# Block sums after the transposes: four transposed blocks in place of seven operands, and the third MLP pair's first products among the first pairs'

## The chip, the cores and the metric

The kernel runs on one core of a Trainium2 chip. The metric is the device time of one execution in microseconds (us), given as the median of several runs; a profiled execution of the same kernel gives the views that are read here. The engines are TensorE (PE; its weight loads are shown as PEld), VectorE (DVE), ScalarE (ACT), GpSimd (POOL) and SyncE (SP), which here issues nearly all transfers. Work of TensorE lands in PSUM, in banks of 128 x 512 float32; everything else lies in SBUF.

## The reference

One decoder block in float32: x is 1024 tokens by 1024 channels.

```python
proj = x @ w_in                      # 1024 x 7168: q, f, i, og, pool_v, gate_a, gate_b
a = HGRN2(q, f, i) -> per-head RMSNorm * sigmoid(og) -> @ w_a
b = per-group linear(causal_mean_w(pool_v) - pool_v) * pool_scale
mix = (sigmoid(gate_a) * a + sigmoid(gate_b) * b) @ w_out
x = LN(alpha * x + mix)
x = LN(alpha * x + relu(x @ w_up)^2 @ w_down)
```

HGRN2 is a gated recurrence over the tokens, 8 heads of 128 channels. The up projection of the MLP has 4096 columns.

## The kernel before, in words

**Seven products for eight.** Each large product of x is computed in the form of Strassen and Winograd. The tokens are split in two halves of 512, the channels in two halves of 512. So x is four blocks a11, a12 (first tokens) and a21, a22 (second tokens). Four sums are formed: s3 = a11 - a21, s2 = a22 - s3, s1 = a21 + a22, s4 = a12 - s2. A pair of output blocks then needs seven half-size products, with a11, a12, s3, a22, s2, s1 and s4, in place of eight (`pair`, with the parts p1 to p7 for the products and t1 to t4 for the sums of weight blocks).

**Precision.** A float32 operand is split into a high part, which ScalarE casts (`A.copy`, fp32r), and a low part, which VectorE gets by subtraction. Three products, high by high, high by low and low by high, make one product (`prod`, `three`). So each operand tile of 128 x 512 costs one ScalarE and one VectorE instruction, and each product of 512 x 128 x 512 costs twelve TensorE instructions.

**Transposes.** Tokens lie on the partitions as loaded, and a product wants the channels there. `transposed_parts` (line 152) turns four 128 x 128 squares into one PSUM bank by four TensorE transposes (line 156), and `split_into` (lines 117 and 118) splits it straight from there into an operand tile. `first_tokens` does so for a11 and a12, `second_tokens` for s3, a22, s2, s1 and s4. The sums are made before the transposes, in `row_sums`, on rows of tokens (lines 169 to 182), one generator per tile of 128 tokens; it yields between the sums so that they can be placed among other work.

**The two stages with x as operand.** The first stage, about the first 96 us, projects the values i. There the weights move and x stands as the stationary operand; products go down four chains of PSUM banks (`onto_chain`) or row by row through the two "hg" banks (`by_rows`). Sums of rows are placed by `summed()` between the products. After it come the heads, with gates and pooling in between, and the products with w_a and w_out. The second stage begins where the layer norm ends (about 800 to 906 us): `mix` forms rows of the sum, norms them and stores them, `row_sums` follows for tiles 4 to 6 directly and for tile 7 later, then the MLP's pairs of hidden units start. The first two pairs go through the seven products together (`run_second`), because each new operand has just become ready; the other fourteen run one after another. The third pair's weight blocks lie in a pool, `fw`, that opens when the pool of rows closes, and its results take rooms there (`spare`).

**Order.** Instructions are written in the program's order and a planner places them on each engine; `tc.issue_after` holds instructions behind another one, `tc.high_priority` draws them forward. Each engine, SP's queue of transfers too, runs its own instructions strictly in the order so made. `ps_tile(tag)` hands out PSUM banks: four "pj", two "hg", two "tr".

Of the kernel before, what the change touches and what calls it, by code (L numbers as in the profile page):

```python
# [16 lines left out]
P = 128  # L17
# [25 lines left out]
def tile_hybrid_block(  # L43
# [40 lines left out]
    def act_tile():  # L84

        return act.tile([P, 2, HALF], F32R, tag="act", name=nm("act"))
# [65 lines left out]
    def transposed_parts(tiles, off, name, kp, tag):  # L152

        ps = ps_tile(tag, 2)
        for c in range(CH):
            done = PE.transpose(ps[:, c * P : (c + 1) * P], tiles[c][:, off + kp * P : off + (kp + 1) * P], ident)  # L156
# [4 lines left out]
    s3_rows = [None] * CH  # L161

    def row_sums(t):


        a11, a12 = r[t - CH][:, :HALF], r[t - CH][:, HALF:]
        a21, a22 = r[t][:, :HALF], r[t][:, HALF:]
        if s3_rows[t - CH] is None:
            V.tensor_add(s1_rows[t - CH], a21, a22)
            s3_rows[t - CH] = a21  # L170
            own = False
        else:
            s1_rows[t - CH] = a21
            own = True
        s3 = s3_rows[t - CH]
        yield V.tensor_sub(s3, a11, a21).ins
        V.tensor_sub(a11, a22, s3)
        yield
        if own:
            V.tensor_add(a21, a21, a22)  # L180
        yield
        V.tensor_sub(a12, a12, a11)
        yield

    def first_tokens(*names):
        for name in names:
            for kp in range(CH):
                transposed_parts(r[:CH], HALF if name == "a12" else 0, name, kp, "tr")

    def second_tokens(name, *tags):  # L190
        where = dict(s2=(r[:CH], 0), s3=(s3_rows, 0), s1=(s1_rows, 0), a22=(r[CH:], HALF), s4=(r[:CH], HALF))
        tiles, off = where[name]
        return [transposed_parts(tiles, off, name, kp, tags[kp % len(tags)]) for kp in range(CH)]
# [66 lines left out]
    def pair(raw, rooms, takes, pz_tag="pj", twin=False):  # L260


        b11, b12, b21, b22 = (raw[kh][:, :, n] for kh in range(2) for n in range(2))
# [36 lines left out]
        def p2(w):  # L300
            ps["c"] = ps_tile()
            prod(ps["c"], w, "a12", True)
# [67 lines left out]
    def run_second(pairs, sums, begun=False):  # L370

        def later(name, *tags, summed=False, after=None):
            def made():
                if summed:
                    with tc.issue_after(made_last[after]) if after else nullcontext():
                        for one in sums:
                            next(one)
                second_tokens(name, *tags)
            return made

        made = (
            ((lambda: None) if begun else later("s3", "tr", "hg", summed=True), later("a22", "tr")),
            (later("s2", "tr", summed=True, after="s3"),), (later("s1", "tr", summed=True, after="a22"),), (later("s4", "tr", summed=True, after="s2"),), (),
        )
        run(*(p[2:] for p in pairs), made=made, behind=(None, "s3", None, None, None))
# [10 lines left out]
    s1_rows = [None] * CH  # L396
    wq = w_scope.enter_context(tc.tile_pool(name="wq", bufs=1, side="right", reuse_waits="tile"))
    with tc.tile_pool(name="xr", bufs=8, side="right", reuse_waits="tile") as xr:
# [5 lines left out]
        ps = ps_tile("tr", 2)  # L404
# [20 lines left out]
        s3_rows[:] = [xr.tile([P, HALF], F32, tag="s3", name=nm("s3"), bufs=CH) for _ in range(CH)]  # L425
# [71 lines left out]
        c11, c21, c22 = ([None] * CH for _ in range(3))  # L497

# [10 lines left out]
        def take_p4(c, ps):  # L509
            c21[c] = c_late()  # L510
            V.tensor_add(c21[c], c22[c], ps)

        def take_p6(c, ps):
            V.tensor_add(c21[c], c21[c], ps)
            put(1, 0, c, c21[c])
# [10 lines left out]
        def made(name):  # L526
            second_tokens(name, "tr")

        sums = [row_sums(t) for t in range(CH, 8)]

        def summed():
            for one in sums:
                next(one)

        first_tokens("a11")
        w = parts(b11)
        first_tokens("a12")
# [4 lines left out]
        made("s3")  # L542
# [5 lines left out]
        made("a22")  # L548
        by_rows(w, "s3", copied(c22, lambda: xr.tile([P, HALF], F32, tag="s3", name=nm("s3"), bufs=CH)))
        with behind_parts("s3"):  # L550
            for k in range(CH):
                V.tensor_add(b22[k], b22[k], b11[k])
                V.tensor_sub(b21[k], b21[k], b22[k])
            w = parts(b21)
            summed()
        made("s2")
        by_rows(w, "a22", take_p4)
        with behind_parts("a22"):
            w = parts(b22)
            summed()  # L560
        made("s1")
        onto_chain(w, "s2", False, take_p6)
        with behind_parts("s2"):
            for k in range(CH):
                V.tensor_sub(b12[k], b12[k], b11[k])
            w = parts(b12)
            again = wide_rows()
            load_block(again, 1, 1)
            b22 = rows_of_block(again)
            summed()  # L570
        made("s4")
# [47 lines left out]
    with tc.tile_pool(name="tmp", bufs=1, side="right", reuse_waits="tile") as tmp:  # L619
# [19 lines left out]
        def head_inputs(h):  # L639
# [23 lines left out]
            ))  # L663
# [278 lines left out]
        nxt = head_inputs(0)  # L942
# [134 lines left out]
    s1_rows[:] = [c_tile() for _ in range(CH - 1)] + [None]  # L1077
    s3_rows[:] = [None] * (CH - 1) + [c_tile()]
    with tc.tile_pool(name="wo", bufs=1, side="right", reuse_waits="tile") as mp:
# [11 lines left out]
        def mix(t, cc):  # L1091
# [22 lines left out]
        first_tokens("a11", "a12")  # L1114
# [18 lines left out]
    with tc.tile_pool(name="up", bufs=1, side="right", reuse_waits="tile") as up:  # L1133
# [15 lines left out]
        def units(i, raw):  # L1149
# [28 lines left out]
            return pair(raw, (c_tile,) * 3, (take(0), last, take(2), take(3)), "hg", i < 2)  # L1178

        def up_blocks(i):  # L1180
            return w_blocks(w_up, i * 2 * P, i * 2 * P + P, (raw_tile, up_raw_tile, lambda: room_raw.pop())[2 if i == 2 else i % 2])
# [5 lines left out]
        sums = row_sums(7)  # L1187
# [11 lines left out]

        room_raw = [ws0[0][:, n : n + 1].rearrange("p m (k n c) -> p (m k) n c", k=CH, n=2) for n in range(2)]  # L1200
        for i in range(2, NP):
            raw, load = up_blocks(i)
            if i == 2:
                spare[:] = [ws0[1][:, n // 2, n % 2 * HALF : (n % 2 + 1) * HALF] for n in range(7)]
# [189 lines left out]
```

## Time and profile before

| | us |
|---|---|
| median of three runs (lowest, highest) | 1477.53 (1477.52, 1479.11) |
| profiled execution | 1482.98 |
| its span, first to last instruction | 1481.3 |
| busy: TensorE, weight loads, VectorE, ScalarE | 1459.1, 1210.8, 1144.8, 746.5 |
| mean granted clock of TensorE | 0.996 |

Rows of a group give the line, the engine, the operation, the tile written and the tiles read, the count, the busy time, the mean of one in ns and the engine's idle time before it, with what ended it. Rows of waits read "engine and its instruction <- what it waited for: us in all, times, longest". Rows of a stretch give its length, then the busy time of PE, PEld, DVE, ACT and POOL with counts, the granted clock, the share of the transfer engines and GB/s. Rows in order of time start with the start and the duration in us; those of the chain of work give start, time on the chain, engine, tile and line.

### The profile page before, as it was taken

Reading aid. Unit: us, or ns where it says so; the run is one execution under the profiler, and the core shown is the slowest. Engines: PE = TensorE matmul, PEld = TensorE weight load, DVE = VectorE, ACT = ScalarE, POOL = GpSimd, SP = SyncE. Lnnn points to the kernel's source line nnn. Section 1 sums busy time; section 2 is a strip of 40 time slices with the busy share of each in tenths; the row PEclk is TensorE's granted clock in tenths of the full one; section 3 lists DMA queues with packets and bytes.
Section 4 is the critical chain, followed back from the end, with each engine's and each line's share of the span. In section 5 each row is a group of like instructions: output and inputs, shape, how many; then the busy total and the mean of one; then the engine's idle time right before and its main releaser. Section 6 shows DMA issues by size and latency. Waiting matters only on the chain.

```text
span 1481.3 us, 20065 instructions
## 1 busy us (share of the span) xinstructions
PE 1459.1 (99%) x7113; PEld 1210.8 (82%) x7113; DVE 1144.8 (77%) x1845; ACT 746.5 (50%) x1365; POOL 63.9 (4%) x244
## 2 busy tenths in 40 slices
PE   8999999999999999999999999999999999999997
PEld 7888888888888887777888887888888888888886
DVE  5867998999998786578985787666666887777977
ACT  4445565665557556355542165555555533343435
POOL 0001110011011010000002100000000100000000
PEclk9999999999999999999999999999999999999999
DMA  6142223233333436996664134444464774545422
GB/s 242 60 140 86 81 85 125 81 95 102 99 114 100 164 124 221 318 296 224 212 198 171 55 102 164 145 152 151 157 229 162 283 264 134 165 131 181 129 71 114
DMA packets 159557, 226.79 MB, mean 153 GB/s; under 512 B 11200, under 2 KB 83424, under 8 KB 159456
## 3 DMA queue, kind: packets, MB, share of 16 engines
q1 hardware_dynamic: 157520, 218.93, 44.5%
q0 software_dynamic: 1152, 4.19, 0.7%
q10 hardware_dynamic: 784, 2.38, 0.5%
q8 instruction: 56, 0.92, 0.3%
q14 instruction: 45, 0.37, 0.1%
HBM read 154.16 MB, written 71.30 MB: 152 GB/s over the span
## 4 chain that ended last, share of the span: by engine, by line
PE 93%; DMA 3%; DVE 2%; ACT 1%; issue 1%; SPq 0%; DVEq 0%; ACTq 0%
PE ps_pj L201 16%; PE ps_pj L199 16%; PE ps_pj L200 15%; PE ps_pj L1275 4%; PE ps_pj L1277 4%; PE ps_pj L1276 4%; PE ps_hg L199 2%; PE ps_hg L201 2%; PE ps_hg L200 2%; PE ps_pj L99 2%; PE ps_pj L101 2%; PE ps_pj L100 2%; PE ps_tr L156 1%; PE ps_hg L1275 1%; PE ps_hg L1277 1%; PE ps_hg L1276 1%
## 5 line engine op out<-in xcount | busy, mean ns | idle before, releaser
L199 PE MATMUL ps_pj<-act,w 128*128 128x512 f32 x1072 | 419.8, 394 | 5.3 <-DVE q L725 2.0
L200 PE MATMUL ps_pj<-act,w 128*128 128x512 f32 x1072 | 419.5, 391 | 0.0
L201 PE MATMUL ps_pj<-act,w 128*128 128x512 f32 x1072 | 414.9, 392 | 1.9 <-DVE w L113 1.7
L199 PEld LDWEIGHTS ps_pj<-act,w 128*128 128x128 f32 x1072 | 201.3, 188 | 49.5 <-ACT w L112 2.9
L201 PEld LDWEIGHTS ps_pj<-act,w 128*128 128x128 f32 x1072 | 201.3, 188 | 45.3 <-DVE w L113 4.3
L200 PEld LDWEIGHTS ps_pj<-act,w 128*128 128x128 f32 x1072 | 201.4, 188 | 40.4
L112 ACT CAST w<-t 128x512 fp32r<-128x512 f32 x170 | 104.5, 620 | 128.5 <-PE ps_pj L200 65.5
L112 ACT CAST w<-raw 128x512 fp32r<-128x512 f32 x143 | 88.1, 620 | 117.9 <-PE ps_pj L200 53.7
L113 DVE TENSOR_TENSOR w<-t,w 128x512 fp32r<-128x512 f32 x170 | 115.9, 687 | 34.5 <-ACT w L112 27.7
L113 DVE TENSOR_TENSOR w<-raw,w 128x512 fp32r<-128x512 f32 x143 | 97.7, 688 | 57.3 <-ACT w L112 41.8
L1237 ACT CAST act<-act 128x1024 fp32r<-128x1024 f32 x66 | 67.0, 1050 | 110.9 <-issue 35.0
L1238 DVE TENSOR_TENSOR act<-act,act 128x1024 fp32r<-128x1024 f32 x66 | 79.5, 1221 | 18.8 <-ACT act L1237 18.8
L1276 PE MATMUL ps_pj<-act,act 128*128 128x512 f32 x240 | 92.9, 389 | 0.0
L1277 PE MATMUL ps_pj<-act,act 128*128 128x512 f32 x240 | 92.9, 389 | 0.0
L1275 PE MATMUL ps_pj<-act,act 128*128 128x512 f32 x240 | 92.5, 389 | 0.0
L272 DVE TENSOR_TENSOR c<-c,ps_pj 128x512 f32<-128x512 f32 x95 | 64.6, 680 | 31.4 <-PE ps_pj L201 25.8
L199 PE MATMUL ps_hg<-act,w 128*128 128x512 f32 x160 | 62.8, 397 | 0.5 <-ACT room L268 0.5
L268 ACT COPY c<-ps_pj 128x512 f32<-128x512 f32 x95 | 54.6, 584 | 17.1 <-PE ps_pj L201 14.7
L200 PE MATMUL ps_hg<-act,w 128*128 128x512 f32 x160 | 63.1, 395 | 0.0
L201 PE MATMUL ps_hg<-act,w 128*128 128x512 f32 x160 | 62.8, 392 | 0.0
L813 DVE RECIPROCAL tC<-tA 128x128 f32<-128x128 f32 x64 | 54.6, 909 | 0.0
L117 ACT CAST act<-ps_tr 128x512 fp32r<-128x512 f32 x54 | 31.0, 590 | 46.8 <-PE ps_tr L156 46.7
(361 smaller groups left out, 2707.5 us busy)
## 6 DMA issues: line engine op xcount, KB each, us to landing
h<-c SPq DMA_DIRECT2D x105, 256.0 KB, 2.6
act<-h SPq DMA_DIRECT2D x78, 256.0 KB, 2.9
raw<-in_w_in_dram SPq DMA_DIRECT2D x64, 256.0 KB, 3.4
draw<-in_w_down_dram SPq DMA_DIRECT2D x16, 1024.0 KB, 8.1
raw<-in_w_up_dram SPq DMA_DIRECT2D x30, 512.0 KB, 4.3
raw<-in_w_in_dram SPq DMA_DIRECT2D x18, 512.0 KB, 3.7
hf<-h SPq DMA_DIRECT2D x34, 256.0 KB, 2.9
c<-o SPq DMA_DIRECT2D x24, 256.0 KB, 4.2
```

The costliest lines, as they stand in the source:

```text
L112: A.copy(hi, src)
L113: V.tensor_sub(lo, src, f(hi))
L199: PE.matmul(ps, wh[:, k], th, start=first and k == 0, stop=False, skip_group_check=True)
L200: PE.matmul(ps, wh[:, k], tl, start=False, stop=False, skip_group_check=True)
L201: PE.matmul(ps, wl[:, k], th, start=False, stop=k == CH - 1, skip_group_check=True)
L268: A.copy(t, ps)
L272: V.tensor_add(t, t, ps)
L1237: A.copy(hi, src)
L1238: V.tensor_sub(lo, src, f(hi))
L1275: PE.matmul(ps, hh[:, w], wh, start=fresh and n == 0, stop=False, skip_group_check=True)
L1276: PE.matmul(ps, hh[:, w], wl, start=False, stop=False, skip_group_check=True)
L1277: PE.matmul(ps, hl[:, w], wh, start=False, stop=n == M - 1, skip_group_check=True)
```

## The change

`transposed` now only transposes. `in_parts` splits any tile, in PSUM or SBUF, into an operand. `first_tokens` transposes a11 and a12, splits them and copies them with ScalarE into `xt`. `second_tokens` transposes for s3 (the block a21) and for a22 only; the sums s3, s2, s1 and s4 are formed by VectorE in place on the transposed tiles of `xt` and split from there. `row_sums` and the generators go. In the first stage the transposes of a11 go to the banks "tr", "tr", "hg", "hg" (in the loop over names: all "tr" before) and the idle products at the start take "hg"; results c21 and c22 lie in rows of x that are no longer needed, and three conditions on the order are put on the evacuations of p4 and p6. In the MLP the third pair loads its blocks into the left halves of rows 4 to 7 once these are transposed, its first product runs after the first step of the first two pairs and its second after two more, and its rooms are the right halves of rows.

```diff
-    def transposed_parts(tiles, off, name, kp, tag):
+    def transposed(tiles, off, kp, tag):
         ps = ps_tile(tag, 2)
         for c in range(CH):
             done = PE.transpose(ps[:, c * P : (c + 1) * P], tiles[c][:, off + kp * P : off + (kp + 1) * P], ident)
+        return ps, done.ins
+
+    def in_parts(name, kp, src):
         xp[name][kp] = act_tile()
-        made_last[name], made_hi[name] = (i.ins for i in split_into(xp[name][kp], ps))
-        return done.ins
+        made_last[name], made_hi[name] = (i.ins for i in split_into(xp[name][kp], src))
...
-    def row_sums(t):
...
+    def first_tokens(name, *tags):
+        for kp in range(CH):
+            ps, _ = transposed(r[:CH], HALF if name == "a12" else 0, kp, tags[kp % len(tags)])
+            in_parts(name, kp, ps)
+            A.copy(xt[name == "a12"][kp], ps)

     def second_tokens(name, *tags):
...
+        a11, a12, s = xt
+        for kp in range(CH):
+            if name in ("s3", "a22"):
+                ps, done = transposed(r[CH:], HALF if name == "a22" else 0, kp, tags[kp % len(tags)])
+                turned.append(done)
+            if name == "s3":
+                V.tensor_sub(s[kp], a11[kp], ps)
+            elif name == "s1":
+                V.tensor_add(a11[kp], s[kp], a11[kp])
+            elif name == "s4":
+                V.tensor_sub(a12[kp], a12[kp], s[kp])
+            in_parts(name, kp, dict(s3=s, s2=s, s1=a11, s4=a12)[name][kp] if name != "a22" else ps)
+            if name == "a22":
+                V.tensor_sub(s[kp], ps, s[kp])
...
-        run(*(p[2:] for p in pairs), made=made, behind=(None, "s3", None, None, None))
+        run(*(p[2 : 3] for p in pairs), made=made, behind=behind)
+        run(third[:1])
+        run(*(p[3 : 5] for p in pairs), made=made[1:], behind=behind[1:])
+        run(third[1:2])
+        run(*(p[5 :] for p in pairs), made=made[3:], behind=behind[3:])
...
-        ps = ps_tile("tr", 2)
+        ps = ps_tile("hg", 2)
...
-        first_tokens("a11")
+        first_tokens("a11", "tr", "tr", "hg", "hg")
...
-        made("s1")
+        with tc.issue_after(taken["a22", 1]):
+            second_tokens("s1")
         onto_chain(w, "s2", False, take_p6)
-        with behind_parts("s2"):
+        with tc.issue_after(taken["a22", 1]):
             for k in range(CH):
                 V.tensor_sub(b12[k], b12[k], b11[k])
             w = parts(b12)
...
-            summed()
-        made("s4")
+        with tc.issue_after(taken["s2", 1]):
+            second_tokens("s4")
...
-                if CH <= t < 7:
-                    list(row_sums(t))
...
-        run(pairs[0][:2])
-        run(pairs[1][:1])
-        summed = next(sums)
-        with tc.issue_after(summed):
-            turned = second_tokens("s3", "tr", "hg")
-            with tc.issue_after(turned[1]):
-                run(pairs[1][1:2])
-            run_second(pairs, [sums], True)
+        run(pairs[0][1:2])
+        run(pairs[0][:1])
+        turned = second_tokens("s3", "tr", "hg")
+        raw = [r[CH + n][:, :HALF].rearrange("p (k c) -> p k c", c=P) for n in range(4)]
+        for kh, n in ((0, 0), (1, 0), (1, 1), (0, 1)):
+            rows_of = w_up[kh * HALF : (kh + 1) * HALF, (4 + n) * P : (5 + n) * P].rearrange("(k p) c -> p k c", p=P)
+            nc.sync.dma_start(out=raw[2 * kh + n], in_=rows_of)
+        third = units(2, raw)
+        with tc.issue_after(turned[1]):
+            run(pairs[1][:1])
+        with tc.issue_after(turned[3]):
+            run(pairs[1][1:2])
+        run_second(pairs, third)
+        spare[:] = [*xt[2], *(r[t][:, HALF:] for t in range(CH, 8))]
+        run(third[2:])
+        spare.clear()
         rows_scope.close()
```

More of the change, by code (lines that the diff above doesn't have):

```diff
@@ L258, in c_late, with pair @@
         return c_tile(False)
-    def pair(raw, rooms, takes, pz_tag="pj", twin=False):
-        b11, b12, b21, b22 = (raw[kh][:, :, n] for kh in range(2) for n in range(2))
+    def pair(raw, rooms, takes, pz_tag="pj", twin=False, pc_tag="pj"):
+        b11, b12, b21, b22 = raw if len(raw) == 4 else (raw[kh][:, :, n] for kh in range(2) for n in range(2))
         c, ps = {}, {}
@@ L497, in tile_hybrid_block @@
         c11, c21, c22 = ([None] * CH for _ in range(3))
+        taken = {}
         def copied(rooms, room):
@@ L524, in take_p3 @@
             put(0, 1, c, t)
[L526 to L533, printed above, removed]
-        first_tokens("a11")
+        first_tokens("a11", "tr", "tr", "hg", "hg")
         w = parts(b11)
-        first_tokens("a12")
+        first_tokens("a12", "tr")
         onto_chain(w, "a11", True, copied(c11, c_late))
@@ L566, in tile_hybrid_block @@
             w = parts(b12)
+        with behind_parts("s2"):
             again = wide_rows()
@@ L1113, in tile_hybrid_block @@
                 mix(t, cc)
-        first_tokens("a11", "a12")
+        xt[1:] = [r[c][:, :HALF] for c in range(CH)], [r[c][:, HALF:] for c in range(CH)]
+        first_tokens("a11", "tr")
+        first_tokens("a12", "tr")
         for t in range(CH, 8):
```

90 lines of the change are left out of this document (30 added, 60 removed).

## The prediction

> **What bounds the kernel now.** I read the page's shares and slices first, then the list of TensorE's own waits, then busy time by stretch, then the two stretches that the change touches, instruction by instruction.
>
> ```profile
> span 1481.3 us, 20065 instructions
> PE 1459.1 (99%) x7113; PEld 1210.8 (82%) x7113; DVE 1144.8 (77%) x1845; ACT 746.5 (50%) x1365; POOL 63.9 (4%) x244
> PE   8999999999999999999999999999999999999997
> ```
> ```profile
> PE ps_pj L199 <- DVE q L725: 2.0, 1, 2.0
> ...
> PE ps_pj L201 <- DVE w L113: 1.7, 1, 1.7
> ...
> PE ps_hg L470 <- ACT s L502: 0.3, 1, 0.3
> ```
>
> TensorE is busy in 99% of the span, in every slice. The second fence is the top, the third and the last of the twelve waits that it has in the whole kernel; the longest is 2.0 us. So work taken from TensorE shortens the span, unless a stretch is left in which its operands come too late. Whether that happens is read from VectorE, the next busiest, stretch by stretch (columns: PE, PEld, DVE, ACT, POOL, clock):
>
> ```profile
> 28.00:58.00 30.00, 28.93 (x146) 23.47 (x145) 26.55 (x43) 12.23 (x22) 0.00 (x0) 1.00 0.10 36
> 58.00:76.00 18.00, 18.00 (x89) 14.88 (x88) 14.20 (x24) 6.95 (x12) 0.00 (x0) 1.00 0.39 118
> 828.00:856.00 28.00, 28.00 (x134) 23.32 (x133) 22.86 (x41) 5.89 (x11) 2.40 (x1) 1.00 0.23 75
> 856.00:896.00 40.00, 39.96 (x215) 33.01 (x214) 31.50 (x52) 25.79 (x47) 0.00 (x0) 1.00 0.27 82
> ```
>
> VectorE has 12% to spare in 28 to 58, 21% in 58 to 76 and 21% in 856 to 896. ScalarE is far off. Memory does not bind: the DMA share (the column after the clock) is 0.10 to 0.39.
>
> **Removed: transposes.** All transposes of x and of the MLP's input stand on one line of the code; here its instructions in the two stages, and what four of them take on the chain of work that ended last:
>
> ```profile
> 0.00:96.00 96.00, 16.68 (x112) 13.69 (x112) 0.98 0.44 148
> 800.00:906.00 106.00, 16.33 (x112) 13.67 (x112) 1.00 0.30 103
> ```
> ```profile
> 60.46 0.44 PE ps_tr L156 x4
> 60.90 0.94 PE ps_pj L472 x4
> ```
>
> Seven operands of four tiles of four transposes make 112 per stage. The change keeps four blocks (a11, a12, a21, a22), 64 per stage, and makes s3, s2, s1 and s4 by sums of transposed tiles. 96 transposes go: 24 groups of four at 0.44 us, 10.6 us, all on TensorE. (The busy column overlaps neighbours, so I take the chain's 0.44.) A 512-column product takes 0.94 / 4 = 0.235 us there; both prices are start to start.
>
> **Added: ScalarE copies.** Eight copies per stage keep the transposed a11 and a12. They have the form of these casts (count, then busy and mean ns):
>
> ```profile
> L117 ACT CAST act<-ps_tr 128x512 fp32r<-128x512 f32 x54 | 31.0, 590 | 46.8 <-PE ps_tr L156 46.7
> L117 ACT CAST act<-c 128x512 fp32r<-128x512 f32 x28 | 16.5, 620 | 10.4 <-DMA c<-o 5.3 <-DMA c<-s 5.1
> L118 DVE TENSOR_TENSOR act<-ps_tr,act 128x512 fp32r<-128x512 f32 x54 | 36.2, 688 | 17.2 <-ACT act L117 17.1
> L118 DVE TENSOR_TENSOR act<-c,act 128x512 fp32r<-128x512 f32 x28 | 18.4, 687 | 1.2 <-ACT act L117 1.2
> ```
>
> 8 x 0.59 = 4.7 us per stage; in 828 to 856, where the MLP's stand, ScalarE is busy 5.9 of 28 us. Sixteen casts per stage now read SBUF, 0.03 us longer each, 0.5 us. Both cost nothing while ScalarE has this room; without it at most 5.2 us per stage.
> On VectorE reading PSUM or SBUF makes no difference: 688 and 687 ns in the last two rows. [...]
>
> **Moved at the start.** The twelve idle products and the parameters' transpose take their bank from "hg"; all four a11 tiles are transposed before the first product, not one ahead of each quarter.
>
> ```profile
> 9.57 0.77 PE L470 MATMUL ps_pj<-w,act 128*128 128x512 f32 x1
> ```
> ```profile
> 10.92 0.62 ACT L112 CAST w<-b 128x512 fp32r<-128x512 f32 x1 [2.35 <-DMA b<-in_w_in_dram]
> ```
> ```profile
> 5.80:9.20 3.40, 1.59 (x14) 1.31 (x13) 1.02 (x4) 1.10 (x2) 0.31 (x1) 1.00 0.99 353
> 9.20:12.60 3.40, 3.40 (x11) 2.81 (x10) 1.82 (x6) 1.68 (x4) 0.00 (x0) 0.50 1.05 402
> ```
>
> x's third piece is queued on SP ahead of the weight rows that land by 10.9, so the first product slips from 9.57 to between 10.3 and 11.8. But two groups that stood later (0.9 us) are then done, and in the half-clock stretch (the last rows: clock 0.50) they take the place of products. Net between -0.5 (none of the slip is felt) and +1.3 (2.2 less the two groups); I take 0, since the slip is nearest to the time of the two groups moved ahead.
>
> **Moved in the projection (28 to 76).** Six of its 14 groups of transposes go from this stretch: TensorE needs 48 - 6 x 0.44 = 45.4 us, VectorE still 26.55 + 14.20 = 40.8 us (16 sums before and after). Today's waits here:
>
> ```profile
> 31.63 0.66 PE L156 MATMUL ps_tr<-ident,s 128*128 128x128 f32 x4 [0.28 <-DVE act L118]
> 32.82 0.50 PE L470 MATMUL ps_hg<-w,act 128*128 128x512 f32 x1 [0.54 <-DVE c L506]
> ```
> ```profile
> 28.48 2.49 DVE L546 TENSOR_TENSOR raw<-raw,act 128x512 f32<-128x512 f32 x4
> ```
>
> TensorE waits for a bank that VectorE empties behind four differences of weights (2.49 us; 0.60 us an instruction back to back). In the changed order the same four stand before the same evacuation, and TensorE is there sooner. I add 0.6 us. Ends: -0.8 if both waits go, +2.6 if the stretch keeps its 48 us. The two "issue after" conditions on p4's and p6's evacuations replace ones on splits; what is queued behind them (b12's parts, s1, s4) is wanted a product of 48 x 0.235 = 11 us later, so 0.
>
> **Moved in the MLP (856 to 896), the tightest place.** Twelve sums of rows 4 to 6, now ahead of 856 (first and last below), become sums of transposed tiles behind the last row's norm; the third pair's first two products and parts come in too.
>
> ```profile
> 823.29 0.69 DVE L169 TENSOR_TENSOR c<-r 128x512 f32<-128x512 f32 x1 [0.81 <-POOL r L1062]
> ...
> 849.88 0.69 DVE L182 TENSOR_TENSOR r<-r 128x512 f32<-128x512 f32 x1
> ...
> 854.66 1.41 DVE L1056 SCALAR_TENSOR_TENSOR r<-r,lmv,act 128x512 f32<-128x512 f32 x2
> 855.99 0.69 DVE L176 TENSOR_TENSOR c<-r,r 128x512 f32<-128x512 f32 x1
> ```
>
> VectorE: 31.5 + 12 x 0.60 + 6 x 0.60 (the third pair's) = 42.3 us. TensorE: 40.0 - 12 x 0.44 + 36 x 0.235 (three products of the third pair, 12 instructions each) = 43.2 us. The two are level. By deadlines: from 855.99 the changed order puts 34 VectorE instructions up to the first low half of s2 (20.4 us), plus 0.6 for the third pair's blocks and 1.0 for ScalarE's casts, so 878.0. TensorE reaches its product after 8 groups and 76 instructions at 0.235: 855.99 + 3.5 + 17.9 = 877.4, 0.6 late. A like place stands at the third pair's own s3 product, and hand-offs between the two engines that I count as immediate come on top: I take 2.0 us. Ends: 0, and 42.3 / 0.885 - 43.2 = 4.6 us if VectorE is busy only as it is in 28 to 58.
>
> ```profile
> raw<-in_w_in_dram SPq DMA_DIRECT2D x64, 256.0 KB, 3.4
> ```
>
> The third pair's four loads wait on SP for row 4's transposes (857.2) ahead of the first stores of hidden units, which are ready only after that; at 3.4 us they land by 861, when VectorE comes to them. If they take 2 us more, ScalarE's s3 casts queue behind, and the 1.5 us of slack there leaves 0.5.
>
> **Gone at the seam.** Today the third pair's blocks load when the rows' pool closes:
>
> ```profile
> 898.63 0.62 ACT L112 CAST w<-draw 128x512 fp32r<-128x512 f32 x1 [2.90 <-DMA draw<-in_w_up_dram]
> ```
> ```profile
> 898.44 0.39 PE L201 MATMUL ps_pj<-act,w 128*128 128x512 f32 x1
> 899.30 0.50 PE L199 MATMUL ps_pj<-act,w 128*128 128x512 f32 x1 [0.48 <-ACT w L112]
> ```
>
> Start to start 0.86 us, where 0.235 is the rule. With the blocks there since 861 this goes, and I count 0.6 us (0.5 to 0.9, if the restart behind it was slower too). What is late next is VectorE's work above, already priced.
>
> **The clock.** A fall to half clock is the price that small waits can have:
>
> ```profile
> 695.30:698.70 3.40, 1.98 (x7) 0.84 (x5) 3.37 (x7) 2.66 (x6) 0.00 (x0) 1.00 0.87 308
> 698.70:702.10 3.40, 3.35 (x8) 2.67 (x9) 3.40 (x6) 2.04 (x4) 0.00 (x0) 0.50 1.00 291
> ```
>
> A stretch with 1.4 us of idle was followed by 3.4 us at half clock, in which 8 products ran: 1.7 us lost. New waits of 2 us close together could do it once. [...] The row speaks for 1.7, which I keep for the upper end.
>
> **Sum.** -10.6 + 0 + 0.6 + 2.0 - 0.6 = -8.6 us. The profiled execution took 1482.98 us (span 1481.3 and 1.7 around it) and would take 1474.4. The median of the plain runs is 1477.53, 5.4 below the profiled one; with the same offset: 1468.9.
>
> **Rivals.** *All cover holds*: no new wait, today's 0.8 in the projection gone: -10.6 - 0.6 - 0.8, 1465.5. For it: VectorE's spare 21% in 856 to 896; against: level loads there.
> *VectorE sets the pace of the MLP's start*, 4.6 us and one half clock, 1.7: 1468.9 + 2.6 + 1.7 = 1473.2. For it: 90% was its best over 30 us.
> *The projection's gain is not kept*: TensorE's longest waits (the fence above: q, w) are on VectorE, and if its chain goes back to the start, 5.3 - 0.6 = 4.7 us are waited away: 1473.6. Against: at the projection's end VectorE itself waits for TensorE, so it moves forward too:
>
> ```profile
> 84.37 1.37 DVE L113 TENSOR_TENSOR w<-b,w 128x512 fp32r<-128x512 f32 x2 [2.39 <-PE ps_pj L471]
> ```
>
> *Slower*: between 856 and 896 each VectorE instruction waits for a ScalarE cast that waits for it, and VectorE keeps today's 79%: 42.3 / 0.79 - 43.2 = 10.3 us, with 1.7 of clock and the projection's 2.6: -11.2 + 14.6, 1480.9. It decides once new waits pass 11.2 us in all. Against: today's idle there is mostly waiting for transposes that go.
>
> **Chances.** Forecast 0.60 (its own range 1466.5 to 1471.5), all cover 0.13, MLP's pace 0.11, projection's gain lost 0.07, slower 0.09. 0.2%, about what a measurement here tells from none, is 3.0 us. Faster: 0.60 + 0.13 + 0.11 and half of the 0.07, 0.88; within it 0.03; slower 0.09. From 1464.7 to 1475.0 holds all but the slower case and the edges.
>
> **What would show it.** 64 transposes per stage; TensorE's busy time down by some 10 us; between 856 and 896 VectorE above 90%, and waits of TensorE of 1 to 3 us there on s2's low halves or on the third pair's parts; no wait at the seam; the stretch between the two stages the same, only sooner. I am wrong if those waits pass 5 us, if the clock falls to half at a new place, or if the waits on q and w grow.

## The result, and the profile after

The changed kernel takes 1467.32 us (median; 1465.08 to 1470.89) against 1478.89 us of the kernel before (1477.52 to 1480.05) beside it on the same chip: ratio 0.9925, 95% interval 0.9911 to 0.9940. That is 11.6 us or 0.75% faster. Timed again with the experiments, it took 1466.42 us, ratio 0.9914 (0.9901 to 0.9928).

Its profiled execution took 1466.14 us. The head of the page:

```profile
span 1464.4 us, 19910 instructions
PE 1444.3 (99%) x7017; PEld 1199.1 (82%) x7017; DVE 1144.1 (78%) x1845; ACT 754.8 (52%) x1381; POOL 64.0 (4%) x244
```

TensorE has 96 instructions fewer (7017, not 7113) and is busy 14.8 us less; VectorE's count and time stay, ScalarE has sixteen copies more. TensorE is still busy in 99% of the span.

The two kernels issue the same number of 512-column products, 5856, so the n-th product is a mark that both have. I cut both profiles at the starts of the 331st (the projection is over), the 2801st, the 3151st (the MLP's transposes are ahead) and the 3401st product (the seam is behind). Busy time by stretch, columns as in the prediction; before, then after:

```profile
0.00:99.83 99.83, 95.29 (x467) 79.26 (x468) 69.84 (x119) 40.16 (x71) 2.78 (x34) 0.98 0.42 143
99.83:763.63 663.80, 655.97 (x3479) 547.44 (x3478) 551.15 (x1021) 375.11 (x795) 42.37 (x196) 1.00 0.47 150
846.69:914.86 68.17, 67.54 (x332) 54.61 (x330) 53.94 (x89) 38.35 (x70) 0.00 (x0) 1.00 0.40 135
```
```profile
0.00:92.48 92.48, 88.12 (x419) 73.17 (x420) 68.66 (x118) 44.03 (x78) 2.78 (x34) 1.00 0.45 154
92.48:752.37 659.89, 654.40 (x3479) 546.42 (x3478) 552.49 (x1023) 375.47 (x797) 42.39 (x196) 1.00 0.47 151
835.43:897.86 62.43, 61.18 (x283) 50.01 (x282) 55.70 (x94) 38.00 (x70) 0.00 (x0) 1.00 0.40 133
```

The start and the projection are 7.35 us shorter, the MLP's stretch 5.74. The stretch between them, where the change does nothing, is 3.9 us shorter in this pair of profiles; the stretch from the 2801st to the 3151st product is 83.06 us in both. The three make 17 us, while the medians differ by 11.6: the profiled execution of before (1482.98 us) was a long one of its kernel; where it was long is read below, under "The same kernels again".

The transposes' line after, in the two stages: 64 each, where there were 112.

```profile
0.00:96.00 96.00, 8.90 (x64) 7.44 (x64) 1.00 0.45 153
790.00:906.00 116.00, 8.76 (x64) 7.64 (x64) 1.00 0.33 113
```

The tight stretches after; they begin sooner, so the last window is moved by 11 us against the prediction's 856 to 896:

```profile
28.00:58.00 30.00, 29.15 (x143) 23.82 (x142) 29.04 (x48) 14.33 (x26) 0.00 (x0) 1.00 0.10 36
58.00:76.00 18.00, 18.00 (x81) 14.89 (x80) 16.82 (x29) 9.29 (x16) 0.00 (x0) 1.00 0.48 147
845.00:885.00 40.00, 38.75 (x185) 31.50 (x184) 38.55 (x65) 27.08 (x50) 0.00 (x0) 1.00 0.35 110
```

VectorE is now busy 97% of 28 to 58, where it had 12% to spare, and 96% of the MLP's 40 us. All TensorE waits of 0.2 us or more in that stretch, from the list of its waits:

```profile
PE ps_pj L195 <- DVE act L118: 0.5, 1, 0.5
PE ps_hg L194 <- ACT c L263: 0.5, 1, 0.5
PE ps_pj L194 <- ACT act L117: 0.2, 1, 0.2
```

They stand at 867.00, 875.06 and 864.13 us: s2's low half, a bank to be evacuated, and a cast of s2's high half. With the slower step that follows each, they cost 2.0 us from start to start. The added work, by line (L170 the copies, L187 and L182 two of the sums; durations in ns, shortest, median, longest):

```profile
L170 ACT COPY c<-ps_tr x4: 577/588/603, 808.2 to 815.8; 128x512 f32<-128x512 f32 x4
L187 DVE TENSOR_TENSOR r<-ps_tr,r x4: 680/681/682, 856.1 to 865.1; 128x512 f32<-128x512 f32 x4
L182 DVE TENSOR_TENSOR c<-r,c x4: 684/684/684, 869.9 to 871.7; 128x512 f32<-128x512 f32 x4
```

The copy costs the 0.59 us assumed; a sum takes 681 ns out of a bank and 684 out of SBUF, so here a sum out of a bank takes no longer, as before a split did not (688 and 687 ns). The last of s2's sums starts at 865.1, and the wait for its low half ends at 867.00.

The start, instruction by instruction, is where the profile departs most from what was forecast. Timeline of TensorE after (start, duration):

```profile
7.30 0.33 PE L156 MATMUL ps_tr<-ident,x 128*128 128x128 f32 x1
9.24 1.09 PE L156 MATMUL ps_hg<-ident,x 128*128 128x128 f32 x8 [1.62 <-DMA x<-in_x_dram]
10.09 0.47 PE L469 MATMUL ps_pj<-w,act 128*128 128x512 f32 x1
10.41 0.39 PE L470 MATMUL ps_pj<-w,act 128*128 128x512 f32 x1
10.64 0.40 PE L469 MATMUL ps_pj<-w,act 128*128 128x512 f32 x1
```

The first product starts 0.5 us later than before (10.09, not 9.57), but products follow each other by 0.23 us from the second on; before, the first seven (9.57 to 12.27 us) ran at a granted clock of 0.50, 0.43 us apart from the second on.

### The profile page after: what moved, and what is told of

It reads as the page before. It is cut to its first block, busy times and chain, and to the rows that moved or that the text cites. A ratio compares the mean times of both kernels' runs of the same rounds, so it can differ in the third digit from the quotient of the medians.

```text
span 1464.4 us, 19910 instructions
## 1 busy us (share of the span) xinstructions
PE 1444.3 (99%) x7017; PEld 1199.1 (82%) x7017; DVE 1144.1 (78%) x1845; ACT 754.8 (52%) x1381; POOL 64.0 (4%) x244
## 4 chain that ended last, share of the span: by engine, by line
PE 92%; DMA 3%; DVE 2%; ACT 1%; issue 1%; SPq 0%; DVEq 0%; ACTq 0%
PE ps_pj L194 16%; PE ps_pj L196 16%; PE ps_pj L195 16%; PE ps_pj L1271 4%; PE ps_pj L1270 4%; PE ps_pj L1272 4%; PE ps_pj L100 2%; PE ps_pj L101 2%; PE ps_pj L99 2%; PE ps_hg L194 2%; PE ps_hg L196 2%; PE ps_hg L195 2%; PE ps_hg L1271 1%; PE ps_hg L1270 1%; PE ps_hg L1272 1%; DMA c<-s 1%
## 5 line engine op out<-in xcount | busy, mean ns | idle before, releaser
L1271 PEld LDWEIGHTS ps_pj<-act,act 128*128 128x128 f32 x240 | 45.1, 188 | 9.7 <-DVE act L1233 0.4
```

The costliest lines, as they stand in the source:

```text
L1271: PE.matmul(ps, hh[:, w], wl, start=False, stop=False, skip_group_check=True)
```

## The experiments

My theory: the transposes taken off TensorE are the gain, some 5 us per stage, less small new waits on VectorE. The rivals: the gain comes from other edits (start, third pair's place); VectorE sets the pace; one stage's gain is lost later; the profiles differ by clock and luck. The table has the median, the ratio to the kernel before with its interval, and from each profile the three stretches cut at the same products as above (us). The kernels were timed in several comparisons, each with the kernel before beside it, and its median differed: 1479.79 us beside the two single stages, "transposes back" and "third pair late"; 1479.49 beside "changed, second profile", "s2 made three times", "sums on GpSimd" and "start undone"; 1477.59 beside "before, second profile" and the other three. So medians of different comparisons are off by some 2 us against each other; the ratios are not, and where the two readings differ both are given.

| kernel | median | ratio | to the 331st | to the 2801st | 3151st to 3401st |
|---|---|---|---|---|---|
| before | 1478.89 | 1 | 99.83 | 663.80 | 68.17 |
| before, second profile | 1477.93 | 1.0008 (0.9997–1.0018) | 100.06 | 663.66 | 67.46 |
| changed | 1467.32 | 0.9925 (0.9911–0.9940) | 92.48 | 659.89 | 62.43 |
| changed, second profile | 1466.42 | 0.9914 (0.9901–0.9928) | 92.76 | 660.09 | 62.47 |
| projection alone | 1474.01 | 0.9957 (0.9943–0.9971) | 92.59 | 661.36 | 68.24 |
| MLP alone | 1474.11 | 0.9961 (0.9948–0.9973) | 99.94 | 660.48 | 62.44 |
| transposes back, idle | 1477.41 | 0.9981 (0.9972–0.9990) | 98.04 | 659.80 | 66.33 |
| third pair late | 1471.75 | 0.9941 (0.9928–0.9955) | 92.60 | 659.72 | 65.93 |
| third pair loaded early, run late | 1468.15 | 0.9938 (0.9926–0.9949) | 92.26 | 660.81 | 64.55 |
| s2 made three times | 1471.29 | 0.9944 (0.9931–0.9957) | 92.57 | 662.02 | 66.86 |
| sums on GpSimd | 1474.09 | 0.9965 (0.9952–0.9978) | 95.83 | 659.88 | 67.04 |
| start undone | 1469.91 | 0.9929 (0.9917–0.9941) | 96.25 | 660.18 | 62.43 |
| start, parameters' bank undone | 1466.58 | 0.9922 (0.9910–0.9935) | 92.74 | 663.13 | 62.43 |
| start, a11's banks undone | 1468.25 | 0.9938 (0.9926–0.9949) | 93.59 | 662.66 | 62.43 |

### One stage at a time

The projection as changed, with the MLP's stage of before (sums of rows, seven operands transposed, third pair behind the seam); the line that stands for it:

```diff
-        first_tokens("a11", "tr")
-        first_tokens("a12", "tr")
+        first_tokens("a11", "a12")
```

> The change in the projection alone; the MLP's first stage is as before (its seven operands transposed, the third pair's blocks loaded when the rows' pool closes). Main theory (the transposes off TensorE are the gain, 12 groups at 0.44 us per stage): 5.3 less 0.6 of waits, so 4 to 6 us shorter than before, 1473 to 1475 us, with 48 transposes fewer and no change from 76 us on but an earlier start. Rival 'the projection's gain is waited away in the middle of the kernel': within 1.5 us of before, with longer waits on q or w between 100 and 720 us. Rival 'the gain in the profile is the clock's half-speed windows and not the transposes': the middle would gain or lose by 1.7 us a window, and the stretch up to 100 us would show much less than 5 us.

And the reverse: the projection of before, the MLP's stage as changed.

```diff
-        second_tokens("s3", "tr")
+            summed()
+        made("s3")
```

> The change in the MLP alone; the projection is as before. Main theory: 5.3 us of transposes off TensorE, 2.0 of new waits, 0.6 back at the seam, so 3 to 5 us shorter than before, 1474 to 1476 us; its gain and that of the projection alone add up to the whole change's 11 to 12 us within 2 us. Rival 'VectorE sets the MLP's pace': 1 us shorter or less. If the two parts together give much less than the whole, something outside both stages (a start of a later chain, the clock) makes the rest.

Alone they give 5.8 us (1474.01 against 1479.79 beside it) and 5.7 us (1474.11). Together that is 11.5 us, against 11.6 and 13.1 for the whole in its two comparisons: the stages add up within 2 us, and neither loses its gain later. The MLP gives more than the 3 to 5 us expected. In the profiles the stretch that an edit doesn't touch stays within 0.1 us (68.24 and 99.94), and the one that it touches is the changed kernel's (92.59 and 62.44). The rival that the projection's gain is waited away falls.

### The transposes put back

```diff
     def in_parts(name, kp, src):
+        if name in ("s2", "s1", "s4"):
+            idle = ps_tile("tr", 2)
+            for c in range(CH):
+                PE.transpose(idle[:, c * P : (c + 1) * P], ident, ident)
```

> The changed kernel with the 96 transposes put back as idle work: beside the sums of s2, s1 and s4, in both stages, four transposes of the identity per tile into a bank that nobody reads. Sums, copies, splits and the third pair's place stay as changed. Main theory: TensorE pays for them, 24 groups at 0.44 us, less what falls into its new waits of 1 to 2 us: 8 to 11 us longer than the changed kernel, 1475 to 1478 us, nearly the time before. Rival 'the gain comes from the other edits (operands made sooner, third pair moved, fewer splits that wait)': 4 us longer or less. Rival 'VectorE is the bound in both stages': the idle transposes fill waits and cost 3 us or less.

1477.41 us, 10.5 us longer than the mean of the changed kernel's two medians, 1466.9, and 8 to 10 us by the ratios (0.9981 against 0.9925 and 0.9914). Busy time of its two stages:

```profile
0.00:98.04 98.04, 94.75 (x468) 79.38 (x469) 68.74 (x118) 44.05 (x78) 2.78 (x34) 1.00 0.43 148
840.89:907.22 66.33, 66.11 (x332) 55.03 (x331) 57.10 (x96) 38.71 (x70) 0.00 (x0) 1.00 0.41 137
```

The projection pays in full: 98.04 less 92.48 is 5.56 us for 12 groups, 0.46 each. The MLP pays 3.9 us, since its waits shrink from 1.2 us to 0.2 there. So the number of transposes explains most of the difference of the kernels. What is left, 2.4 us to the kernel before beside it (1479.79), is not the transposes: this kernel keeps the changed start, and its 49th product starts at 22.00 us like the changed kernel's, where before it starts at 23.88. VectorE is close to being the bound in the MLP but is not it in the projection.

### The third pair's place

First with its blocks loaded into the down weights' room, and all its products run, behind the seam as before:

```diff
-        run(third[:1])
...
-        run(third[1:2])
...
-        run(third[2:])
...
-        for i in range(3, NP):
+        for i in range(2, NP):
```

> The changed kernel with the third pair back in its old place and its blocks loaded when the rows' pool closes; the sums of transposed blocks stay. Main theory: the seam's wait of 0.6 to 0.9 us comes back, VectorE is freed of the third pair's six instructions between 845 and 885 us, so that its waits of 1 us there go: 0 to 1 us longer than the changed kernel. Rival 'the third pair's move is a gain of its own by covering the wait for s2's sums': 2 to 5 us longer, with new waits of TensorE on s2 or a22 in that stretch. Rival 'the third pair's work overloads VectorE there': 1 us shorter or more.

Then with the loads as changed, but the first two products behind the first pairs' last:

```diff
-        run(third[:1])
-        run(*(p[3 : 5] for p in pairs), made=made[1:], behind=behind[1:])
-        run(third[1:2])
+        run(*(p[3 : 5] for p in pairs), made=made[1:], behind=behind[1:])
         run(*(p[5 :] for p in pairs), made=made[3:], behind=behind[3:])
+        run(third[:1])
+        run(third[1:2])
```

> The changed kernel with the third pair's blocks still loaded early into the rows' rooms, but its first two products run behind the last products of the first two pairs and not among them. Tells the two parts of the 4.9 us that putting the third pair back cost. Theory 'cover' (its products stand where TensorE waits for VectorE's sums and splits): 2.5 to 5 us longer than the changed kernel, with waits of TensorE between 848 and 885 us like those of the kernel with the third pair in its old place. Rival 'seam' (the wait is the late load): within 1 us of the changed kernel.

The old place costs 4.9 us by the medians (1471.75 against 1466.9), 2.4 to 4.0 by the ratios, and 3.5 in the MLP's stretch of the profiles. I had expected 0 to 1; the rival with 2 to 5 held. TensorE's waits there, third pair late, then loaded early and run late:

```profile
PE ps_pj L194 <- ACT w L112: 1.7, 1, 1.7
PE ps_pj L196 <- DVE w L113: 1.3, 2, 0.9
PE ps_pj L194 <- DVE c L267: 0.6, 1, 0.6
```
```profile
PE ps_pj L194 <- ACT w L112: 1.9, 2, 1.7
PE ps_pj L196 <- DVE w L113: 0.4, 1, 0.4
```

In both, TensorE waits 1.7 us for a weight part at about 871 us, which the changed kernel doesn't: the third pair's products stand there and give VectorE the time. That cover is worth 64.55 less 62.43, 2.1 us; the early load another 65.93 less 64.55, 1.4 us. Neither theory of the second run was right alone: the cover is the larger half. By the medians the second kernel is some 1 us (1468.15 against 1466.9), by the ratios some 2 to 3.5 us behind the changed one, which fits 2.1.

### More VectorE work at the tight place

```diff
             if name == "a22":
-                V.tensor_sub(s[kp], ps, s[kp])
+                for _ in range(1 if in_projection[0] else 3):
+                    V.tensor_sub(s[kp], ps, s[kp])
```

> The changed kernel with eight more VectorE instructions at the tightest place: in the MLP, each of s2's four tiles is made by three differences (a22 less s, turned back and forth) and not one, 8 x 0.69 = 5.5 us of VectorE work; TensorE's work and the rest of the kernel stay. Main theory (VectorE and TensorE are level in the 40 us behind the norm): VectorE, busy 38.6 of 40 us there, has some 1.4 us left, so 3 to 5 us longer than the changed kernel, with waits of TensorE on s2's parts. Rival 'VectorE has room there, its busy share is only its early start': 1 us longer or less.

1471.29 us, 4.4 us over the two medians' mean; in the MLP's stretch 66.86 less 62.43, 4.4 us. Its 40 us:

```profile
848.00:888.00 40.00, 35.89 (x166) 28.29 (x164) 39.49 (x67) 25.01 (x46) 0.00 (x0) 1.00 0.29 92
```

VectorE is busy 99% and TensorE 90%. Of 5.5 us of added work (4.8 if the eight take the 0.60 us that an instruction has back to back), 4.4 reach the end. The two engines are level in the changed kernel, as the sum had it.

### Sums on GpSimd

```diff
             elif name == "s1":
-                V.tensor_add(a11[kp], s[kp], a11[kp])
+                G.tensor_add(a11[kp], s[kp], a11[kp])
             elif name == "s4":
-                V.tensor_sub(a12[kp], a12[kp], s[kp])
+                G.tensor_sub(a12[kp], a12[kp], s[kp])
```

> The changed kernel with the sums of s1 and s4 (16 instructions in the two stages) on GpSimd and not on VectorE. Takes 4 x 2 x 0.6 = 4.8 us off VectorE in each stage. Main theory: TensorE's new waits in the two stages, some 3 us together, are on VectorE's chain, so 0 to 2.5 us shorter than the changed kernel, if GpSimd makes a sum in less than 1.5 us. Rival 'the waits are hand-offs of single splits and not VectorE's load': within 1 us. Rival 'GpSimd shares VectorE's way to the buffers and is slow': 1 to 4 us longer, VectorE's instructions beside the sums longer.

1474.09 us, 7.2 us longer, where I had expected it to be 0 to 2.5 us shorter; the rival "slow" had the direction, and 1 to 4 us. Both stages lose, 3.4 and 4.6 us. Groups of GpSimd by line, and two groups of VectorE's timeline beside them:

```profile
L182 POOL TENSOR_TENSOR c<-r,c 128x512 f32<-128x512 f32 x4 | 6.1, 1517 | 37.2 <-DVE r L187 37.2
L184 POOL TENSOR_TENSOR x<-x 128x512 f32<-128x512 f32 x4 | 8.9, 2217 | 0.0
```
```profile
870.94 0.68 DVE L187 TENSOR_TENSOR r<-ps_tr,r 128x512 f32<-128x512 f32 x1
872.33 3.45 DVE L118 TENSOR_TENSOR act<-r,act 128x512 fp32r<-128x512 f32 x2
```

By these groups a sum takes 1.5 to 2.2 us on the mean, and two VectorE instructions beside it take 3.45 us, where two of the same line take 1.29 in the changed kernel (at 25.97 us). The work taken off VectorE this way came back to it longer; what lengthens VectorE's instructions there is not shown.

### The start

The whole start undone, then each half of it:

```diff
-        ps = ps_tile("hg", 2)
+        ps = ps_tile("tr", 2)
...
-        first_tokens("a11", "tr", "tr", "hg", "hg")
+        first_tokens("a11", "tr")
```

> The changed kernel with the start's banks as before: the twelve idle products and the parameters' transpose take a bank of the transposes, and all four a11 tiles are transposed through those banks alone. Theory of the prediction (the start moves by -0.5 to +1.3 us, taken as 0): within 1 us of the changed kernel; the first product of the projection starts up to 0.5 us sooner or later than 10.09 us. Rival 'the changed start is a gain, because the transposes no longer wait for the banks': 1 to 3 us longer.

> The changed kernel with one half of the start's edit undone: the idle products and the parameters' transpose take a bank of the transposes again; a11 keeps its four banks, so that all four tiles can still be transposed ahead of the first product. Theory 'the shared bank makes the half clock' (the second group of transposes waits 1.8 us for the parameters' copy, as in the kernel before, and the clock falls for 3.4 us behind it): a stretch at half clock at 9 to 13 us again, 1 to 2.5 us longer than the changed kernel. Rival 'all four tiles ahead of the first product are what counts': full clock, within 0.7 us of the changed kernel.

> The changed kernel with the other half of the start's edit undone: a11's tiles go through the two banks of the transposes alone, so that the third and fourth groups stand behind the first quarters' products; the idle products keep their bank of the products. Theory 'the shared bank makes the half clock': full clock at 9 to 13 us, and 0 to 2 us longer than the changed kernel, by the wait of some 1.2 us for a12's parts that the kernel with the whole start undone showed at 23 to 26 us. Rival 'all four tiles ahead count': 2 to 4 us longer, as with the whole start undone, and the half clock at 9 to 13 us.

Undone as a whole the start costs 3.5 us beside the changed kernel in the same comparison (1469.91 against 1466.42), and 3.8 us in the profile (96.25 less 92.48), which is outside what I had allowed. Undoing the parameters' bank alone changes nothing that can be told (1466.58; 92.74), undoing a11's banks alone costs 1.1 us in the profile (93.59; 1468.25). So the theory "the shared bank makes the half clock" fell as I put it: each half alone kept the full clock, in one profile each. Busy time and clock by stretch, the whole start undone, then the parameters' bank alone. Within a profile the stretches at half clock begin whole multiples of 3.413 us apart (the two of the kernel before are 3.413 us long each in the clock records of its trace and begin 689.49 us apart, 202 times that), at another time in each execution (9.19 us in the kernel before, 9.42 with the start undone), and each fence is cut at the times of its own profile:

```profile
6.00:9.42 3.42, 1.66 (x15) 1.38 (x14) 1.17 (x6) 1.10 (x2) 0.31 (x1) 1.00 1.04 360
9.42:12.83 3.41, 3.41 (x11) 2.73 (x10) 2.56 (x7) 2.58 (x6) 0.00 (x0) 0.50 1.05 401
```
```profile
4.81:8.22 3.41, 1.90 (x16) 1.62 (x15) 1.26 (x2) 1.72 (x3) 0.31 (x1) 1.00 1.00 334
8.22:11.64 3.42, 2.60 (x18) 2.39 (x19) 1.91 (x8) 1.32 (x4) 0.00 (x0) 1.00 1.04 385
```

All four profiles with the old start (before twice, the MLP alone, the start undone) have 3.4 us at half clock from 8.9 to 9.4 us on, and none of the ten others has. So cut, the emptiest window of the start, from 3.4 us on, holds 1.5 to 1.7 us of busy TensorE in these four and 1.9 to 2.9 in the ten. But later in the kernel that does not separate them; the kernel before, then the start undone:

```profile
623.58:626.99 3.41, 1.60 (x8) 0.98 (x6) 0.74 (x2) 0.00 (x0) 0.00 (x0) 1.00 1.08 383
626.99:630.41 3.42, 3.27 (x14) 2.74 (x15) 2.65 (x5) 1.12 (x2) 0.00 (x0) 1.00 1.07 387
```
```profile
688.68:692.09 3.41, 2.14 (x8) 1.00 (x7) 3.41 (x7) 3.15 (x6) 0.00 (x0) 1.00 0.92 292
692.09:695.50 3.41, 3.41 (x10) 2.67 (x9) 3.41 (x7) 1.66 (x3) 0.00 (x0) 0.50 0.94 311
```

A window with 1.60 us busy was followed by the full clock, one with 2.14 by half. What else sets the fall off, and whether the old start would have been spared in an execution whose steps of 3.413 us lie elsewhere, stays open.

### The same kernels again

> The changed kernel once more, unchanged, for the spread of the profile: the profile of the changed kernel had no stretch at half clock ahead of the last 5 us, that of the kernel before had two (9 to 13 and 699 to 702 us). Theory 'the stretches at half clock go with the place in the run, not with the kernel': this profile differs from the first by one or two such stretches, 1.7 us each, and the plain times spread by 5 us again with the granted clock (0.998 to 0.997). Rival 'the change took the cause of the half clock away': again none, and the plain times gain 3 us more than TensorE's work lost.

> The kernel before once more, for a second profile. Its first profile took 1482.98 us, 3 to 5 us over the median of its plain runs. Theory 'the stretch between the stages (100 to 820 us) is not changed, and the 3.9 us that the two first profiles differ there are this profile's own waits': between the 331st and the 2801st 512-column product this profile takes 2 to 4 us less than the first one of this kernel, and its half clock at 9 to 13 us is there again. Rival 'the change also shortens the middle': the same stretch again 3 us longer than in the changed kernel's two profiles.

The second profile of the changed kernel has no half clock ahead of its last 5 us either, and its stretches agree with the first within 0.3 us. The second of before agrees with the first too, but for 0.7 us in the MLP's stretch: it took 1484.57 us, with 663.66 us in the middle and the half clock at the start (0.54 in the row below, which is cut at the first profile's times; its own stretch begins at 8.88).

```profile
9.20:12.60 3.40, 3.14 (x10) 2.71 (x11) 2.53 (x10) 1.72 (x4) 0.00 (x0) 0.54 1.04 387
```

So my expectation of 2 to 4 us less in the middle was wrong for the profile. The starts of the products show where the middles part. From the 331st product to the 2052nd all fourteen profiles agree within 0.03 us, and from the 2621st to the 2801st within 0.01. The whole difference arises between, at 571 to 712 us of the changed kernel. Up to the 2516th product the same few waits of TensorE are longer or shorter: 3.0 of the 3.9 us by which the first profile of before is behind, among them the wait for q (2.0 us, 0.3 in the changed kernel). Then six profiles have a stretch at half clock, at 691 to 699 us: before twice, the MLP alone, and the three kernels with the start undone in whole or half. From the 2516th to the 2621st product they take 0.8 to 1.8 us more than the first profile of the changed kernel, 0.9 in the first of before; the other eight lie between 1.0 less and 0.4 more.

The work there is the same in all, and in the first profiles of the kernel before and of the changed one it also stands in the same order on each engine, at other times (from 140 to 755 us before: 3261 matmuls on TensorE, 974 instructions on VectorE, 756 on ScalarE, 185 on GpSimd, 334 on SP): the kernel with the parameters' bank undone has 663.13 us, the MLP alone 660.48 although its clock fell. So a middle of 660 or of 663.5 us is met by executions with the same work, and why the waits differ is not shown. Both profiled executions of before lie 4 to 7 us above the medians of its plain runs, at a granted clock of 0.996 where most plain runs have 0.997 to 0.999. That these mostly have the short middle is argued from the sum (7.35 + 5.74 = 13.1 us in the two stages, 11.6 and 13.1 by the medians), and isn't seen in a trace.

No kernel tried beats the changed one; the one with the parameters' bank undone equals it.

## Why the prediction was right, step by step

Forecast 1468.9 us, measured 1467.32: 11.6 us of gain where 8.6 were forecast. The two times lie closer together (1.6 us) than the two gains (3.0), because the forecast started from 1477.53 us and the kernel before took 1478.89 beside the changed one; that much of the agreement is luck.

**Transposes, -10.6.** Right: 0.46 us a group in the projection and, with the waits that it filled (1.0 us fewer), about 0.41 in the MLP, by putting them back.

**ScalarE's copies, 0.** Right: 588 ns each, ScalarE at 27 of 40 us in the MLP's tight stretch, and no wait of TensorE on a copy.

**The start, 0, between -0.5 and +1.3.** This step failed. The slip of the first product (0.5 us) and the two groups moved ahead were as described, but I kept the stretch at half clock as given. With the slip of 0.5 and the two groups' 0.9 alone the term would have been -0.4. But the half clock went, and with it the delay of seven products, some 1.5 us together: at the 49th product the changed kernel is 1.9 us ahead, though until there it has as many transposes to do. This is read from the profiles; how many plain runs of before have that stretch isn't shown.

**The projection, +0.6.** From the 49th to the 331st product it gains 5.5 us, where 5.3 less 0.6 were forecast. VectorE runs at 97% there, but the 0.6 of new waits did not come: the waits for its evacuations stay as long as before.

**The MLP, +2.0.** Right in size, 2.0 us, with VectorE at 96%, and partly in place: s2's two halves make most of it, but the wait for a bank was not forecast. The experiment with more VectorE work shows that the engines are level. What I missed is that the third pair's products, which I booked as load (0.6 us of VectorE each), stand where TensorE would wait: without them 2.1 us more.

**The seam, -0.6.** Mis-sized, by 0.4 to 1.0. Before, TensorE's products from 898.44 on:

```profile
898.44 0.39 PE L201 MATMUL ps_pj<-act,w 128*128 128x512 f32 x1
899.30 0.50 PE L199 MATMUL ps_pj<-act,w 128*128 128x512 f32 x1 [0.48 <-ACT w L112]
899.64 0.40 PE L200 MATMUL ps_pj<-act,w 128*128 128x512 f32 x1
900.03 0.50 PE L201 MATMUL ps_pj<-act,w 128*128 128x512 f32 x1
900.37 0.39 PE L199 MATMUL ps_pj<-act,w 128*128 128x512 f32 x1
...
903.82 0.50 PE L201 MATMUL ps_pj<-act,w 128*128 128x512 f32 x1
904.16 0.40 PE L199 MATMUL ps_pj<-act,w 128*128 128x512 f32 x1
```

Only the first gap is listed as a wait, but the steps behind it are 0.34, 0.39 and 0.34, where those from 900.37 to 902.66 are 0.22 to 0.24, and two more restarts follow at 903. From 898.44 to 904.16 there are 18 products; at 0.23 us they take 4.1 us, and they took 5.7. So the seam was worth 1.6 us in this profile; in the second of before the restarts at 903 are missing, the same 18 products take 5.1 us, and it was worth 1.0. Loading early alone gave 1.4.

With -1.9 for the start, -5.5 for the projection and -5.7 for the MLP with its seam, the sum is -13.1 by the first profiles, -12.3 by the second ones (7.30 and 4.99 us), and -11.6 and -13.1 by the medians. The forecast was short by 4.5 us of the first sum: the start (1.9), the seam (1.0) and the waits of the projection (0.8). The other 0.8 us lies in the MLP's stretch, and no step accounts for it.

**The clock.** No fall at a new place in the changed kernel: its clock of 0.50 begins at 1459.24 us, in its last 5. That the price exists is shown by the kernel with the sums on GpSimd, where a wait of TensorE in the MLP reached 2.3 us: the rows there, cut at 3.41 us.

```profile
871.03:874.44 3.41, 1.08 (x5) 0.60 (x4) 3.41 (x4) 2.75 (x6) 3.41 (x3) 1.00 0.40 110
874.44:877.85 3.41, 3.41 (x9) 2.64 (x8) 3.41 (x3) 2.59 (x5) 2.48 (x2) 0.50 0.33 115
```

TensorE was busy 1.08 of 3.41 us, and the next 3.41 us ran at 0.50: 8 products at 0.43 us and not 0.23, an estimate of 1.6 of the 4.6 us that this stretch lost. With the start undone, 1.66 us of the 3.42 before the fall were busy (all of it with instructions of 128 columns or fewer). So neither fall came behind a stretch that was idle throughout.

**The rivals.** "All cover holds" (1465.5) was nearest among them, but for another reason: the waits came, and start and seam gave more. VectorE's pace, the lost projection and the slower case aren't seen in any run.

## What to carry to other kernels

Where one engine was busy 99% of the time, a removed instruction was worth its time on that engine (0.46 us a group of four transposes in the projection, about 0.41 in the MLP), provided that the next engine had the time, which is read stretch by stretch and not over the span; here it left that engine 3 to 4% in both stages, and that was just enough. Work of the busy engine that needs little from the level one (the third pair's products) belongs where the operands come late: that place was worth 2.1 us here. A wait is to be sized from the starts of the products around it and not from the listed idle time: here 1.2 us listed in the MLP cost 2.0, and 0.48 listed at the seam cost 1.6 (0.45 cost 1.0 in the second profile), by the slower steps behind each restart.

## What the hardware did that I had not expected

Two stretches at half clock in the same profile lie 202 times 3.413 us apart (from 9.19 to 698.68 us in the kernel before; 202 times again in its second profile, 201 in the MLP alone, from 9.08 to 695.16, and 200 with the start undone, from 9.42 to 692.09). So in these four profiles they fit a grid of 3.413 us, and the grid lies elsewhere in each. Idle time alone doesn't tell whether one comes: behind a window with 1.60 us busy the clock stayed (the kernel before, 623.58 us), behind one with 2.14 it fell (the start undone, 688.68 us). With the sums on GpSimd, a 128x512 sum takes 1.5 to 2.2 us there on the mean against 0.68 on VectorE, and two VectorE instructions beside it took 3.45 us and not 1.29. After waits of 0.48 to 0.52 us the first product took 0.50 us and the next followed by 0.34, not 0.23 (at 899.30 us in the kernel before, at 867.00 and 875.06 in the changed one).
